# A decoder layer step: the recurrence's mean of squares as two split products

## The chip, the cores and the metric

The kernel runs on one core of a Trainium2 chip. The metric is device time in microseconds (us), the median of several runs; before the change it is 869.17 us (three runs, 868.96 to 870.31). Besides, one execution is recorded by the hardware profiler; all durations of single instructions come from that one.

## What is computed

One inference step of a decoder layer on 256 prompt tokens and 8 x 8 sample tokens, 320 rows of 2048. One projection of the rows feeds three groups of heads: sparse attention (8 heads, with an indexer that picks the keys, and pages of cached keys and values for the sample tokens), a gated linear recurrence (4 heads), and cross attention into memory (4 heads). Each branch is gated, the branches are concatenated and go through an output projection and a layer norm. The change concerns the recurrence's norm, which the reference writes so (`b_o` is the recurrence's output, 128 values a head and token):

```
bn = b_o * lax.rsqrt(jnp.mean(b_o * b_o, axis=-1, keepdims=True) + RMS_EPS) * norm_g
b = bn.reshape(n_b, n_t, W_B) * jax.nn.silu(bg)
```

## The kernel before

**The large products.** Activations stand transposed, features on the 128 partitions, the 320 tokens along the free axis. A float32 weight block (128x512) is split in two: ScalarE casts it to float32r (`wh`, line 626), VectorE or GpSimd subtracts to get the remainder (`wl`, lines 628 and 630). Each product is then three float32r matmuls, high by high, high by low, low by high (lines 1643 to 1645). In the profile these are the rows `pj<-xh,wh`, `pj<-xl,wh` and `pj<-xh,wl`. Other products, among them those of the recurrence, multiply float32 operands directly.

**The order.** Nearly every instruction passes through one helper (line 155), so the profile gives that line for all, and groups are told apart by tiles: `pj` are the projections' sums, `kv` and `va` the page visits' (scores and values), `mA` and `mB` the sums of the smaller stages, `t` and `bp` work buffers in SBUF, `pg` and `S` pages. While the program is built, a planner (class `Plan`, line 57, and the loop from line 2054) keeps an estimate of when each engine is free and each tile is ready. The branches' stages are generators (`bg`); at a `yield need(...)` a stage stops until the plan says that its operands are there, at `room` until a buffer is free, at `wait` until another stage has reported itself in `done`. Between the stages' steps the loop gives TensorE the next page visit (`unit`) or the next six matmuls of a projection (`pe_quantum`). `TT` (line 296) puts an elementwise operation on VectorE or on GpSimd, whichever the plan says is done first. The order within each engine is thus settled when the program is built, and every engine executes its own in that order.

**The recurrence** (`hgrn`, line 1333) treats its four heads one after the other. A head takes both large buffers `bp` (lines 1339 and 1340), transposes its values into the buffer `vN` (128x384, line 1346), builds decays and scores, then frees the two buffers and takes them again for the state `S0` and the sample tokens' values `vx` (line 1427). The decayed keys go into `kN` (128x256, line 1494). The head's output is formed in one sum `po` (lines 1522 to 1528), copied to `oT`, and squared by ScalarE into `sq` (line 1532). Eight updates of the state follow on VectorE (line 1540), the state is stored and its buffers freed (line 1543). The mean of the squares over the 128 partitions is a product with a constant matrix `onesm` whose entries are all 1/128 (line 1547), in float32. It leaves the mean in every partition. Lines 1549 to 1556 make the inverse root and scale.

`vN`, `kN` and `onesm` are single buffers; `onesm` is filled by a GpSimd memset at the start (line 1884). The masks' setup (`masks`, line 1926) runs after the indexer.

**The cross queries** of the sample tokens (`pad_queries`, line 439) need one `bp` buffer: it is cleared on GpSimd, ScalarE copies four heads' queries into it, and the visits `XK` to the memory keys read it. It is freed after the last visit `XV` (line 762).

Of the kernel before, what the change touches and what calls it, by code (L numbers as in the profile page):

```python
# [10 lines left out]
F32 = mybir.dt.float32  # L11
F32R = mybir.dt.float32r
# [4 lines left out]
OP = mybir.AluOpType  # L17
# [9 lines left out]
NS, NT = 64, 320  # L27
# [193 lines left out]
def need(*aps, ps=1, lag=0.0, visit=0.0):  # L221

    return (aps, ps, lag, visit)
# [3 lines left out]
def hymba_step(ctx: ExitStack, tc: tile.TileContext, I, O):  # L227
    nc = tc.nc
    plan = Plan()
    PE, ACT, DVE, POOL, SP = (Engine(plan, n, e) for n, e in (  # L230
        ("PE", nc.tensor), ("ACT", nc.scalar), ("DVE", nc.vector), ("POOL", nc.gpsimd), ("SP", nc.sync)))
# [7 lines left out]
    def new(shape, tag, dt=F32, p=None):  # L239
        uid[0] += 1  # L240
        bufs = BUFS.get(tag, 1)
        t = (p or pool).tile(shape, dt, name=f"{tag}_{uid[0]}", tag=tag, bufs=bufs)
        plan.slot(tag, bufs, t.tensor.name)
        if tag in ("t", "bp"):
            live[t.tensor.name] = [tag, 1]
        return t
# [7 lines left out]
    def free(*ts):  # L254
        for t in ts:
            e = live.get(t.tensor.name)
            if e:
                e[1] -= 1
                if e[1] == 0:
                    del live[t.tensor.name]  # L260

    def has_room(k, tag="t", spare=0):
        return sum(e[0] == tag for e in live.values()) + k + spare <= BUFS[tag]

    def room(k, tag="t", spare=0):
        while not has_room(k, tag, spare() if callable(spare) else spare):
            yield

    def const(shape, name, dt=F32):
        return pool.tile(shape, dt, name=name, tag=name, bufs=1)  # L270

    def T(cols=NT, dt=F32):
        return new([128, cols], "t", dt)
# [16 lines left out]
    def PS(shape, which=None, dt=F32):  # L290
        if which is None:
            fa, fb = [(held[w] == 2, plan.slot_free(w, 2)) for w in ("mA", "mB")]
            which = "mA" if fa <= fb else "mB"
        return new(shape, which, dt, psum)

    def TT(op, out, a, b):
        n = math.prod(out.shape[1:])
        d = max(plan.t["DVE"], plan.now) + (66 + n) / 960 + hold_dve[0]
        p = max(plan.t["POOL"], plan.now) + (170 + 2.0 * n) / 960
        (DVE if d <= p else POOL).tensor_tensor(out, a, b, op=op)  # L300
# [4 lines left out]
    def spare():  # L305
        return 0 if AQ else 0

    def store(dst, src):
        keep(src)
        outq.append((dst, src))  # L310
# [4 lines left out]
    ident = const([128, 128], "ident")  # L315
# [9 lines left out]
    ngt = const([128, 1], "ngt")  # L325
    eps = const([128, 2], "eps")
    one = const([128, 1], "one")
    onesm = const([128, 128], "onesm")
    emat = const([128, 2, 2, 2, 128], "emat", BF)
    pbias = const([128, 384], "pbias")  # L330
    maskb = const([128, HALF], "maskb", BF)
# [15 lines left out]
    done = set()  # L347
# [89 lines left out]
        return f  # L437

    def pad_queries():
        yield from wait(("mq", 0))  # L440
        yield from room(1, "bp")
        st["mqpad"] = x = new([128, 8, 4, 32], "bp")
        POOL.memset(x, 0.0)
        for h in range(4):
            yield from wait(("mq", h))
            q = st.pop(("mq", h))
            yield need(q, ps=0)
            ACT.copy(x[:, :, h, 8 * h:8 * h + 8], q[:, 256:320].rearrange("p (b t) -> p b t", b=8))
            free(q)
        done.add("mqpad")  # L450
# [363 lines left out]
    def wait(*keys):  # L814
        while not all(k in done for k in keys):
            yield
# [516 lines left out]
    def hgrn():  # L1333
        lb, olb = lbt[:, 8:12], lbt[:, 12:16]
        yield from wait("idxdone", "pbias", "masks")
        for h in range(4):
# [9 lines left out]
            vN = new([128, 3, 128], "vN")  # L1346
            ps = PS([128, 3, 128])
# [141 lines left out]
            ps = PS([128, 3, 128])  # L1489
# [1 line left out]
                PE.transpose(ps[:, i, :], kd[:, 128 * i:128 * i + 128], ident)  # L1491
            PE.transpose(ps[:, 2, :], kd[:, 192:320], ident)
            free(kd)
            kN = new([128, 2, 128], "kN")
            ACT.copy(kN, ps[:, 0:2])
            yield from room(3, spare=spare)
            kS = T(256, F32R)
# [6 lines left out]
            ps = PS([128, 2, 128])  # L1504
# [8 lines left out]
            for a in range(2):  # L1513
                for j in range(4):
                    PE.matmul(pq[32 * j:32 * j + 32, a, :], q[:, 256 + 32 * a:288 + 32 * a], S0[:, 4 * a + j, :],
                              start=True, stop=True)
# [13 lines left out]
            oT, sq = at, x  # L1530
            ACT.copy(oT, po)
            ACT.activation(sq, po, AF.Square)
            for a in range(2):
                yield need(vx, kS)
                ps = PS([128, 4, 128])
                PE.matmul(ps, kS[:, 0:128], vx[:, 4 * a:4 * a + 4, :], start=True, stop=False)
                PE.matmul(ps, kS[:, 128:256], vx[:, 4 * a:4 * a + 4, :], start=False, stop=True)
                for b in range(4):
                    e = 1 + 4 * a + b
                    DVE.scalar_tensor_tensor(S0[:, 4 * a + b, :], S0[:, 4 * a + b, :], eG[:, e:e + 1], ps[:, b, :],  # L1540
                                             op0=OP.mult, op1=OP.add)
            store(O["ss"][h], S0)
            free(S0, vx, kS)
            yield from room(1, spare=spare)
            yield need(sq)
            ps = PS([128, NT])
            PE.matmul(ps, onesm, sq, start=True, stop=True)
            y = T()
            ACT.activation(y, ps, AF.Ln, bias=eps[:, 0:1])
            ACT.activation(y, y, AF.Exp, scale=-0.5)  # L1550
# [330 lines left out]
        nc.tensor.matmul(warm_ps, warm[:, 0:128], warm, start=True, stop=True)  # L1881
    free(warm)
    POOL.memset(avS[0:64], 0.0)
    POOL.memset(onesm, 1.0 / 128)
    POOL.memset(one, 1.0)
    POOL.memset(eps[:, 0:1], RMS_EPS)
    POOL.memset(eps[:, 1:2], LN_EPS)
# [38 lines left out]
    def masks():  # L1926
        yield from wait("idxdone")
        yield from room(2, "bp")
        cm = [new([128, 1024], "bp"), new([128, 1024], "bp")]
        SP.dma_start(lbt[:, 0:8], I["lb"])  # L1930
        SP.dma_start(ngt, I["ng"])
        SP.dma_start(cm[0], I["cm"][:, 0:1024])
        SP.dma_start(cm[1], I["cm"][:, 1024:2048])
        yield need(*cm, lbt, ngt)
        ACT.copy(cu8, cm[0][:, 0:304])
        ACT.copy(emat.rearrange("p a b c d -> p (a b c d)"), cm[1])
        free(*cm)
        DVE.tensor_scalar(ngt, ngt, -0.5, None, op0=OP.mult)
        l0, l1, m = lbt[:, 0:4], lbt[:, 4:8], lbt[:, 8:12]
        DVE.tensor_max(m, l0, l1)  # L1940
        DVE.tensor_sub(l0, l0, m)
        DVE.tensor_sub(l1, l1, m)
        yield
        ACT.activation(lbt[:, 0:8], lbt[:, 0:8], AF.Exp)
        DVE.tensor_add(m, l0, l1)
        DVE.reciprocal(m, m)
        DVE.tensor_mul(lbt[:, 8:12], l0, m)
        DVE.tensor_scalar(lbt[:, 12:16], lbt[:, 8:12], -1.0, 1.0, op0=OP.mult, op1=OP.add)
        done.add("masks")


    for g in (setup(), masks(), idx_head(), idx_sample(), attn_scores(), attn_values(), *[new_keys(p) for p in range(4)],
              *[soft(p) for p in range(4)], hgrn(), pad_queries(), *[cross_prompt(h) for h in range(4)], split()):
        bg.append([g, None])
# [99 lines left out]
    while half < len(wspec) or bg or outq or later_in or pending or nunit < len(punits):  # L2054
        plan.now = max(plan.now, plan.t["PE"])
        loads()
        if pending and pending[0][0] is mem_values and has_room(4, spare=spare()):
            f, ps, _ = pending.pop(0)
# [8 lines left out]
        while pending and plan.avail(pending[0][1] if pending[0][2] == 3 else pending[0][1][-1]) <= plan.now \  # L2067
# [3 lines left out]
            f, ps, _ = pending.pop(0)  # L2071
# [138 lines left out]
```

## Time and profile before

| what | value |
|---|---|
| median of three runs | 869.17 us |
| lowest and highest | 868.96 and 870.31 us |
| the profiled execution's own time | 868.29 us |
| its span, first to last instruction | 866.5 us |
| mean granted TensorE clock | 0.998 |
| memory read and written | 256.50 and 8.73 MB |

The span is 1.79 us shorter than the time of the same execution. In the profile, PE is TensorE's matmuls and PEld its weight loads, DVE VectorE, ACT ScalarE, POOL GpSimd, SP the engine that issues most DMAs. A row of a timeline has start, duration, engine, line, operation, the tiles written and read, shape and number of instructions merged (`x2`); in square brackets stand the idle time before it and what ended it. A row of a group has busy time and mean duration in ns behind the bar, then idle time before these instructions and what ended most of it. A row of waits has who waited for whom, the time in total, how often, and the longest. Matmuls overlap, so their durations add up to more than the time that they take together.

### The profile page before, as it was taken

Reading aid. Unit: us, or ns where it says so; the run is one execution under the profiler, and the core shown is the slowest. Engines: PE = TensorE matmul, PEld = TensorE weight load, DVE = VectorE, ACT = ScalarE, POOL = GpSimd, SP = SyncE. Lnnn points to the kernel's source line nnn. Section 1 sums busy time; section 2 is a strip of 40 time slices with the busy share of each in tenths; the row PEclk is TensorE's granted clock in tenths of the full one; section 3 lists DMA queues with packets and bytes.
Section 4 is the critical chain, followed back from the end, with each engine's and each line's share of the span. In section 5 each row is a group of like instructions: output and inputs, shape, how many; then the busy total and the mean of one; then the engine's idle time right before and its main releaser. Section 6 shows DMA issues by size and latency. Waiting matters only on the chain.

```text
span 866.5 us, 19303 instructions
## 1 busy us (share of the span) xinstructions
PE 856.6 (99%) x6972; PEld 729.7 (84%) x6974; DVE 555.4 (64%) x1133; ACT 422.7 (49%) x900; POOL 299.1 (35%) x305
## 2 busy tenths in 40 slices
PE   9999999999999999999999999999999999999996
PEld 8999998888888998887878889677887789888885
DVE  6777989645888895563484448558635344953655
ACT  6444566544454545343463454555445353744432
POOL 0453553356544463040142213333411000623424
PEclk9999999999999999999999999999999999999999
DMA  8555644889999999999999999999999987856633
GB/s 306 185 176 159 183 140 129 326 310 371 398 384 385 346 358 363 363 377 406 380 350 399 400 367 381 403 405 362 379 372 395 373 334 257 297 174 195 194 98 122
DMA packets 84370, 266.51 MB, mean 308 GB/s; under 512 B 10609, under 2 KB 21810, under 8 KB 83634
## 3 DMA queue, kind: packets, MB, share of 16 engines
q1 hardware_dynamic: 83250, 263.18, 82.6%
q0 software_dynamic: 1024, 2.10, 0.8%
q8 instruction: 55, 0.90, 0.4%
q14 instruction: 41, 0.34, 0.1%
HBM read 256.50 MB, written 8.73 MB: 306 GB/s over the span
## 4 chain that ended last, share of the span: by engine, by line
PE 97%; DVE 1%; DMA 1%; SPq 0%; issue 0%; ACT 0%; DVEq 0%
PE pj L155 57%; PE mB L155 12%; PE va L155 10%; PE mA L155 10%; PE kv L155 8%; DMA pg<-in_xT 1%; DVE pg L155 0%; DVE t L155 0%; DVE s L155 0%; SPq L155 0%; DVE xl L155 0%; ACT xh L155 0%; DVE wl L155 0%; DVEq L2196 0%; DVE bns L155 0%
## 5 line engine op out<-in xcount | busy, mean ns | idle before, releaser
L155 ACT CAST wh<-wr 128x512 fp32r<-128x512 f32 x338 | 207.4, 619 | 255.7 <-PE pj L155 203.4
L155 PE MATMUL pj<-xh,wh 128*128 128x320 f32 x1008 | 322.0, 319 | 0.0
L155 PE MATMUL pj<-xh,wl 128*128 128x320 f32 x1008 | 311.5, 309 | 0.0
L155 PE MATMUL pj<-xl,wh 128*128 128x320 f32 x1008 | 311.3, 309 | 0.0
L155 DVE TENSOR_TENSOR wl<-wr,wh 128x512 fp32r<-128x512 f32 x239 | 181.9, 770 | 190.8 <-ACT wh L155 183.3
L155 POOL TENSOR_TENSOR wl<-wr,wh 128x512 fp32r<-128x512 f32 x99 | 131.8, 1335 | 235.4 <-ACT wh L155 217.9
L155 PEld LDWEIGHTS pj<-xh,wh 128*128 128x128 f32 x1008 | 189.4, 188 | 18.2 <-issue 13.5
L155 PEld LDWEIGHTS pj<-xl,wh 128*128 128x128 f32 x1008 | 189.5, 188 | 1.4
L155 PEld LDWEIGHTS pj<-xh,wl 128*128 128x128 f32 x1008 | 189.2, 188 | 0.0
L155 POOL TENSOR_TENSOR t<-t,t 128x320 f32<-128x320 f32 (+3 forms) x44 | 39.5, 898 | 129.6 <-ACT t L155 68.2
L155 PE MATMUL kv<-pg,qpad 128*32 128x256 f32 (+1 forms) x916 | 59.2, 380 | 0.0
L155 PE MATMUL va<-pg,PT 128*32 128x512 f32 x456 | 58.5, 595 | 0.0
L155 PEld LDWEIGHTS kv<-pg,qpad 128*32 128x32 f32 (+1 forms) x916 | 31.5, 110 | 21.1 <-issue 1.9
L155 DVE MAX8 PT<-PT 128x8 f32<-128x1032 f32 x32 | 39.5, 1233 | 0.5
L155 DVE MATCH_REPLACE8 PT<-PT 128x1032 f32<-128x1032 f32 x32 | 39.0, 1218 | 0.0
L155 PEld LDWEIGHTS va<-pg,PT 128*32 128x32 f32 x456 | 14.6, 109 | 29.0 <-issue 26.3
L155 POOL DMA_INDIRECT S<-in_ci,row x24 | 26.0, 1084 | 31.6 <-DVE row L155 22.0
L155 POOL TENSOR_TENSOR t<-t,tabm 128x320 f32<-128x320 f32 x16 | 14.1, 879 | 34.2 <-DVE t L155 32.6
L155 PE MATMUL mB<-t,wh 128*128 128x256 f32 x128 | 24.5, 290 | 0.0
L155 POOL TENSOR_TENSOR xl<-cat,xh 128x256 fp32r<-128x256 f32 x12 | 13.4, 1142 | 27.2 <-ACT xh L155 27.2
L155 POOL TENSOR_TENSOR bp<-t,bp 128x128 f32<-128x128 f32 (+1 forms) x17 | 10.4, 615 | 35.4 <-ACT bp L155 35.3
L155 ACT ACTIVATE S<-kv 128x512 f32<-128x512 f32 x16 | 9.5, 596 | 26.4 <-PE kv L155 23.2
(378 smaller groups left out, 1348.9 us busy)
## 6 DMA issues: line engine op xcount, KB each, us to landing
wr<-in_wt SPq DMA_DIRECT2D x126, 512.0 KB, 6.0
pg<-in_ck SPq DMA_DIRECT2D x114, 512.0 KB, 7.1
pg<-in_cv SPq DMA_DIRECT2D x114, 512.0 KB, 7.3
wr<-in_wo SPq DMA_DIRECT2D x36, 512.0 KB, 4.4
wr<-in_wm SPq DMA_DIRECT2D x16, 512.0 KB, 8.1
S<-in_ck SPq DMA_DIRECT2D x14, 512.0 KB, 6.8
S<-in_cv SPq DMA_DIRECT2D x14, 512.0 KB, 6.9
pg<-in_cXK SPq DMA_DIRECT2D x8, 512.0 KB, 9.4
```

Source lines behind the costliest of these rows:

```text
L155: res = f(*a, **k)
```

## The change

The squares are split into a float32r part `sh` and a float32r remainder `sl`, and the float32 product with `onesm` becomes two float32r products into one sum. No new buffers are made for the parts: `sh` takes the single buffer of the head's values (`vN`), `sl` that of its keys (`kN`), which becomes 128x320 for it. `onesm` becomes float32r, and is now written by a VectorE instruction in the masks' setup instead of the memset. The third head reports `states` when its state's buffers are free, and `pad_queries` waits for that besides the first cross query. ("Third" counts from zero: it is the last.)

```
-    onesm = const([128, 128], "onesm")
+    onesm = const([128, 128], "onesm", F32R)
...
     def pad_queries():
-        yield from wait(("mq", 0))
+        yield from wait(("mq", 0), "states")
         yield from room(1, "bp")
...
-            kN = new([128, 2, 128], "kN")
+            kN = new([128, NT], "kN")[:, 0:256].rearrange("p (a b) -> p a b", a=2)
...
             ACT.copy(oT, po)
             ACT.activation(sq, po, AF.Square)
+            sh, sl = new([128, 384], "vN", F32R)[:, 0:NT], new([128, NT], "kN", F32R)
+            ACT.copy(sh, sq)
+            TT(OP.subtract, sl, sq, sh.bitcast(F32))
...
             free(S0, vx, kS)
+            if h == 3:
+                done.add("states")
             yield from room(1, spare=spare)
-            yield need(sq)
+            yield need(sh, sl)
             ps = PS([128, NT])
-            PE.matmul(ps, onesm, sq, start=True, stop=True)
+            PE.matmul(ps, onesm, sh, start=True, stop=False)
+            PE.matmul(ps, onesm, sl, start=False, stop=True)
...
-    POOL.memset(onesm, 1.0 / 128)
...
+        DVE.tensor_scalar(onesm, ident, 0.0, 1.0 / 128, op0=OP.mult, op1=OP.add)
```

## Prediction

> **What bounds the kernel now.** I read the page first: its busy times, its forty slices and the chain that ended last.
>
> ```profile
> span 866.5 us, 19303 instructions
> PE 856.6 (99%) x6972; PEld 729.7 (84%) x6974; DVE 555.4 (64%) x1133; ACT 422.7 (49%) x900; POOL 299.1 (35%) x305
> PE 97%; DVE 1%; DMA 1%; SPq 0%; issue 0%; ACT 0%; DVEq 0%
> ```
>
> TensorE is busy for 99% of the span and carries 97% of the chain. Matmuls overlap, so "busy" alone could hide waiting; hence the second view, who TensorE waited for, asked for that engine alone. Its two longest rows:
>
> ```profile
> PE kv L1881 <- DVE t L155: 1.1, 1, 1.1
> PE mB L155 <- DVE t L155: 0.3, 1, 0.3
> ```
>
> The first is the start of the program; after it TensorE waits next to nothing. The third view is busy time by stage, for the stretch in which the recurrence works and the one around its end:
>
> ```profile
> 350.00:650.00 300.00, 299.93 (x2847) 244.13 (x2849) 169.54 (x354) 144.91 (x321) 80.64 (x98) 1.00 1.00 382
> 650.00:716.00 66.00, 65.73 (x524) 50.86 (x523) 30.11 (x75) 30.75 (x79) 6.35 (x6) 1.00 0.93 362
> ```
>
> The columns are the stretch's length, then PE, PEld, DVE, ACT and POOL busy, the granted clock, the DMA share and GB/s. TensorE fills both stages (299.93 of 300.00 us, 65.73 of 66.00), at a granted clock of 1.00. The DMA engines are full too from 350 to 650, but no wait of TensorE's comes of it, since projections stand ready between the page visits. So what counts is the time for which TensorE's stream is occupied; work on the other engines counts only if it makes that stream wait or puts it into another order.
>
> **The change part by part.** *The product itself.* Before, each head multiplies the squares by a constant 128x128 matrix in full float32. The tile view of that constant, two rows of it:
>
> ```profile
> L155 PE MATMUL mA<-t,onesm x6: 431/432/433, 509.9 to 680.2; 128*128 128x320 f32 x6
> L155 PE MATMUL mB<-t,onesm x2: 432/432/433, 433.9 to 434.2; 128*128 128x320 f32 x2
> ```
>
> Eight instructions for four heads: one product of the program is two on the engine. What it occupies is not the 432 ns (instructions overlap) but the distance between starts, in TensorE's timeline around the second head, and in a piece of the chain that holds projections alone:
>
> ```profile
> 509.61 0.31 PE L155 MATMUL pj<-xl,wh 128*128 128x320 f32 x1
> 509.75 0.31 PE L155 MATMUL pj<-xh,wl 128*128 128x320 f32 x1
> 509.90 0.70 PE L155 MATMUL mA<-t,onesm 128*128 128x320 f32 x2
> 510.20 0.55 PE L155 MATMUL pj<-xh,wh 128*128 128x320 f32 x1
> 510.59 0.31 PE L155 MATMUL pj<-xl,wh 128*128 128x320 f32 x1
> ```
>
> ```profile
> 718.25 22.88 PE pj L155 x156
> ```
>
> From the last projection matmul before it (509.75) to the second one after it (510.59) are 0.84 us. That holds two projection matmuls, 128x128 by 128x320 in float32r, which otherwise follow each other at 22.88 / 156 = 0.147 us. So the full float32 product takes 0.84 - 2 x 0.147 = 0.55 us. After the change it is two float32r products of the projections' shape: 2 x 0.147 = 0.29 us. Saved: 0.25 us a head, 1.0 us for four. This is the first term, and it lies on TensorE, on the path.
>
> Does the stream of matmuls set that distance, or the loading of their weights? The loads' timeline at the same place:
>
> ```profile
> 509.61 0.19 PEld L155 LDWEIGHTS pj<-xh,wl 128*128 128x128 f32 x1
> 509.76 0.34 PEld L155 LDWEIGHTS mA<-t,onesm 128*128 128x128 f32 x2
> ```
>
> There are two loads a product before and two after. Loads of 0.19 us stand 0.15 us apart, so they overlap one another, and 0.34 us of loads do not explain a product of 0.55 us. I take the stream as the limit, and 1.0 us as the term. The Trainium skill's "Perfetto Trace Analysis", in its section Identifying the Most-Contended Engine, would have TensorE's distance from its limit judged by the share of the weight loads and not by busy matmuls. By that measure, 84% here and untouched by the edit, the term would be nothing, and the sum the old time. The steady 0.147 us under loads of 0.19 speak against it here.
>
> *The split.* Each head gets a cast of the squares on ScalarE (line 1532's result into the buffer of the values) and a subtraction on VectorE or GpSimd. The nearest groups by form, of the same shape and number types, then the two ends for the constant:
>
> ```profile
> L155 ACT CAST PT<-S 128x320 fp32r<-128x320 f32 x4 | 1.8, 457 | 1.1 <-DMA S<-in_wik 1.1
> L155 DVE TENSOR_TENSOR cat<-S,PT 128x320 fp32r<-128x320 f32 x4 | 1.9, 486 | 2.6 <-ACT PT L155 2.6
> L155 POOL TENSOR_TENSOR t<-t,t 128x320 f32<-128x320 f32 x19 | 17.3, 910 | 71.8 <-DVE t L155 24.7 <-PE pj L155 17.3 <-ACT t L155 14.9
> L155 DVE TENSOR_SCALAR pbias<-pbias 128x128 f32<-128x128 f32 x1 | 0.2, 228 | 0.0
> L155 POOL MEMSET onesm<- 128x128 f32 x1 | 0.2, 198 | 0.0
> ```
>
> So 4 x 0.46 = 1.8 us more on ScalarE (49% busy), and 4 x 0.49 = 1.9 us more on VectorE (64%) or 4 x 0.91 = 3.6 us on GpSimd (35%). The constant moves from a 0.2 us memset at the program's start to a 0.2 us VectorE instruction in the masks' setup, after the indexer. All of this runs beside TensorE's stream: I put it at nothing, with the stream's other work as its cover.
>
> *What the split delays.* The head's own chain is longer by 0.46 + 0.49 = 0.94 us, or 0.46 + 0.91 = 1.37 us with GpSimd. Here is head 3: ScalarE's square,
>
> ```profile
> 678.55 0.45 ACT L155 ACTIVATE t<-mB 128x320 f32<-128x320 f32 x1
> ```
>
> then VectorE's first four state updates and TensorE's product:
>
> ```profile
> 678.75 1.12 DVE L155 SCALAR_TENSOR_TENSOR bp<-bp,eG,mA 128x128 f32<-128x128 f32 x4 [0.61 <-PE mA L155]
> ...
> 679.89 0.70 PE L155 MATMUL mA<-t,onesm 128*128 128x320 f32 x2
> ```
>
> The square ends at 679.00 and the product starts at 679.89, so 0.89 us of the extra 0.94 to 1.37 are there already; the rest only moves the product behind some projection matmuls, because the planner issues it when its estimate says that both parts are there. Behind the subtraction on VectorE stand the eight state updates: the first starts at 678.75 now and at 679.00 + 0.94 = 679.94 then, 1.2 us later. Who waits for those: the state's store and the release of two large buffers, and then the cross queries.
>
> *The parts' buffers.* They take the values' and keys' single buffers, whose readers (the keys' and values' products) stand before the square in the same head; the next head's copy into them stands after the product. I see no new wait in that, at worst one that the sequence of the head has anyway.
>
> *The wait for the states.* The cross queries' buffer is one of the two large ones, both held by head 3 until its states are done. ScalarE's rows of head 3's first exponentials and of the first cross query's copy, GpSimd's of the clearing of its buffer, ScalarE's of the last query's copy, and the chain's piece with the visit that reads them:
>
> ```profile
> 594.57 0.83 ACT L155 ACTIVATE t<-t 128x320 f32<-128x320 f32 x2
> ...
> 617.37 0.42 ACT L155 COPY t<-pj 128x320 f32<-128x320 f32 x1
> ...
> 683.19 0.95 POOL L155 MEMSET bp<- 128x1024 f32 x1
> ...
> 686.70 0.24 ACT L155 COPY bp<-t 128x64 f32<-128x64 f32 x1
> ...
> 697.09 3.59 PE kv L155 x64
> ```
>
> Head 3 holds both buffers from 594.57; the first cross query is there at 617.37, 23 us later; the buffer is cleared at 683.19, after the states. The new wait is thus one that already takes place, and costs nothing. With the states 1.2 us later the padded queries are there at some 688.1 instead of 686.94, still 9 us ahead of the visit at 697.09 that needs them. And if that visit slipped, the 22.88 us of projections from 718.25, with no visit among them, are there to fill the stream. Without that cover each microsecond of delay would cost one.
>
> The sum: 868.29 us (profiled execution: span 866.5 and 1.79 around it) - 1.01 = 867.28. That execution lies 0.88 under the median of the runs, 869.17; carried over to it, 869.17 - 1.01 = 868.16, my forecast 868.2. The runs before span 0.16%; I take 0.2% (1.74 us) as what can be told from no change.
>
> **The unknown cost** is the order. The kernel's order is planned by estimated times; from the masks on every estimate of VectorE shifts by a fraction of a microsecond, from the first head on TensorE's and ScalarE's too, and choices made by a comparison may fall otherwise. Two prices for that, TensorE's timeline at a product whose operand came later than planned, and at the entry into a page visit:
>
> ```profile
> 651.26 0.33 PE L155 MATMUL mB<-ident,t 128*128 128x128 f32 x1
> 651.87 0.55 PE L155 MATMUL mB<-ident,t 128*128 128x128 f32 x3 [0.27 <-DVE t L155]
> ...
> 681.17 0.31 PE L155 MATMUL pj<-xh,wl 128*128 128x320 f32 x1
> 681.41 1.92 PE L155 MATMUL va<-pg,PT 128*32 128x512 f32 x16
> ```
>
> The late operand cost 0.61 us between two starts where a transpose needs under 0.2 (three end within 0.55), so 0.4 to 0.5; a visit's entry takes 0.24 instead of 0.147, 0.1, and I allow as much for its exit. A handful of each, either way, is an estimate of 1 to 2.3 us of either sign. I take zero, since nothing in the trace favours a sign.
>
> **The rivals.** *The gain does not arrive* (0.10): TensorE is limited by loading weights or by the pages, and the product's shortening is filled with waiting. For it: DMA at 1.00 from 350 to 650, and two weight loads a product before and after, the measure that "Perfetto Trace Analysis" would go by. Against it: the loads overlap, as shown, and TensorE lacks 0.07 us of 300 in just that stretch, so it waits for no page. The time would be the old one, 869.2.
>
> *The order falls better* (0.28): two late operands fewer, or some visits merged, bring 0.8 to 2.3 us beyond the term: 865.9 to 867.4, faster.
>
> *TensorE stands at the product* (0.06): its queue is in order, and if a part is later than the plan thinks, the projections behind it wait. Each head loses its gain at 0.25 us of such waiting; over 0.2% slower needs (1.74 + 1.01) / 4 = 0.69 us in each. If cast and subtraction lay wholly on TensorE's path, 4 x 1.37 = 5.5 us: 868.2 + 5.5 = 873.7. Against it: the planner waits for both parts, and the error of its estimates seen above is 0.5 us, in a single place.
>
> *The order falls worse* (0.05): 2.8 us or more lost, six late operands: 870.9 or over.
>
> **How the numbers follow.** The forecast, order about kept, has the remaining 0.51. Faster by over 0.2% (under 867.4) is the better order: 0.28. Within 0.2%: forecast and lost gain, 0.61. Slower: the standing product and the worse order, 0.11. The range is the forecast with 2.3 us of order below and 2.4 above: 865.9 to 870.6. It leaves out the tails of the last two rivals and some of the better order, about 2 in 10. The forecast's own part is about 867.5 to 868.9.
>
> **What would show it.** In the profile after: the matmuls with the constant still eight, but at 0.15 us between starts, 0.25 us less a head from the projection before to the one after; the cast at about 0.46 us and the subtraction at 0.49 or 0.91; first state update about 1.2 us after the square; the clearing of the cross buffer right behind the states; TensorE still at 99%, the pieces of pure projections at the end about as long. Wrong I would be if TensorE's row of waits shows the constant's product with a wait of 0.3 us or more, if the page visits split into more pieces than before, or if the stream of TensorE has the same or a greater sum of gaps than the 1 us saved.

## The result, and the profile after

The changed kernel takes 874.51 us, the median of five runs (872.73 to 875.23), beside 869.17 us for the kernel before on the same chip: ratio 1.0055, 95% interval 1.0043 to 1.0066. It is 5.3 us slower, and lies outside the range of the prediction, on the side that had a chance of 0.11. The profiled execution took 874.51 us, its span is 872.7 us. (Other chips gave the kernel before 867.85, 869.64 and 868.09 us. So experiments are compared by their ratio to runs of before on their own chip.)

The page, with the lines that answer to the first ones of before, shows little: TensorE is still busy for 98% of the span, but 6.2 us of span have come on top.

```profile
span 872.7 us, 19322 instructions
PE 858.7 (98%) x6972; PEld 731.0 (84%) x6974; DVE 559.0 (64%) x1125; ACT 423.2 (49%) x904; POOL 312.5 (36%) x317
PE 94%; DVE 2%; POOL 1%; issue 1%; DMA 1%; ACT 1%; SPq 0%; DVEq 0%; POOLq 0%; ACTq 0%
```

The second view, who TensorE waited for, has a row that before has not:

```profile
PE mB L155 <- ACT t L155: 3.3, 1, 3.3
PE kv L1887 <- DVE t L155: 1.1, 1, 1.1
PE pj L155 <- DVE wl L155: 0.8, 1, 0.8
```

The third row, a wait at 86 us ahead of all of the change's work, is no part of the change (see the last section); it adds about 1 us to the difference between these two profiles. The first row is the one that counts: a single wait of 3.3 us. It is not at the product over the squares, but at matmuls that write a bank `mB`. TensorE's timeline at that place, of the kernel after:

```profile
612.66 0.31 PE L155 MATMUL pj<-xh,wl 128*128 128x320 f32 x1
616.30 0.55 PE L155 MATMUL mB<-ident,t 128*128 128x128 f32 x3 [3.33 <-ACT t L155]
616.60 0.43 PE L155 MATMUL pj<-xh,wh 128*128 128x320 f32 x1
616.83 0.46 PE L155 MATMUL pj<-xl,wh 128*128 128x320 f32 x1
617.09 0.47 PE L155 MATMUL pj<-xh,wl 128*128 128x320 f32 x1
...
620.02 0.41 PE L155 MATMUL pj<-xl,wh 128*128 128x320 f32 x1
620.27 0.31 PE L155 MATMUL pj<-xh,wl 128*128 128x320 f32 x1
620.42 0.32 PE L155 MATMUL pj<-xh,wh 128*128 128x320 f32 x1
```

The three merged instructions are head 3's transposes of its values (line 1346 and after). They stand at the head of TensorE's queue, which is in order, and projections that need nothing from them stand behind. Two things are to be seen. First the stop itself. Second, what follows it: projection matmuls that start every 0.147 us elsewhere start every 0.266 us from 616.83 to 620.27, 13 of them, which is 13 x 0.12 = 1.55 us more. The busy time by stage says why (length, PE, PEld, DVE, ACT and POOL busy, then the granted clock):

```profile
612.00:617.00 5.00, 1.67 (x12) 1.41 (x11) 4.69 (x8) 2.58 (x8) 2.73 (x2) 0.98 0.81 269
617.00:624.00 7.00, 7.00 (x40) 7.00 (x39) 2.29 (x2) 2.10 (x5) 2.57 (x2) 0.77 0.94 293
```

In the seven microseconds behind the stop TensorE is full, and its granted clock is 0.77, where it was 1.00 in the stages of before. Stop and slow stretch are 3.3 + 1.55 = 4.9 us of the 5.3.

What did the transposes wait for? The other engines' timelines in those microseconds:

```profile
612.24 1.37 DVE L155 TENSOR_TENSOR wl<-wr,wh 128x512 fp32r<-128x512 f32 x1 [1.48 <-ACT wh L155]
613.53 1.54 DVE L155 SCALAR_TENSOR_TENSOR t<-t,ngt,t 128x320 f32<-128x320 f32 x1
...
615.42 0.75 DVE L155 COPY t<-mB 128x256 f32<-128x256 f32 x2
...
615.87 0.70 ACT L155 COPY t<-mB 128x256 f32<-128x256 f32 x2 [2.42 <-DVE t L155]
...
611.76 2.96 POOL L155 TENSOR_TENSOR wl<-wr,wh 128x512 fp32r<-128x512 f32 x2 [2.19 <-ACT wh L155]
```

The four copies `t<-mB` move the memory keys out of the two banks `mB`, which the memory projection has just filled. VectorE makes two of them, and is late. Beside GpSimd's splitting of weights its own split takes 1.37 us instead of 0.69, and the gate's step 1.54, where one of its shape at 608 us takes 0.55. ScalarE's two copies come behind VectorE's. Only then is a bank free for the transposes. In the kernel before, the same transposes stood 17 us earlier, in the other kind of bank:

```profile
595.36 0.49 PE L155 MATMUL mA<-ident,t 128*128 128x128 f32 x3
```

And the product that the change is about? Here is head 1's, in TensorE's timeline of after:

```profile
511.69 0.31 PE L155 MATMUL pj<-xh,wl 128*128 128x320 f32 x1
511.84 0.31 PE L155 MATMUL mA<-vN,onesm 128*128 128x320 f32 x1
511.99 0.31 PE L155 MATMUL mA<-kN,onesm 128*128 128x320 f32 x1
512.14 0.31 PE L155 MATMUL pj<-xh,wh 128*128 128x320 f32 x1
512.29 0.31 PE L155 MATMUL pj<-xl,wh 128*128 128x320 f32 x1
```

From 511.69 to 512.29 are 0.60 us, where before had 0.84 between the same neighbours: 0.24 us less, as forecast. So the loss does not come from the product's price. The orders of all engines are the same as before up to head 0's product at 434 us (but for the constant's write) and differ from there on.

### The profile page after: what moved, and what is told of

Its sections match the earlier page's. It is cut to its first block, busy times and chain, and to the rows that moved or that the text cites. A ratio compares the mean times of both kernels' runs of the same rounds, so it can differ in the third digit from the quotient of the medians.

```text
span 872.7 us, 19322 instructions
## 1 busy us (share of the span) xinstructions
PE 858.7 (98%) x6972; PEld 731.0 (84%) x6974; DVE 559.0 (64%) x1125; ACT 423.2 (49%) x904; POOL 312.5 (36%) x317
## 4 chain that ended last, share of the span: by engine, by line
PE 94%; DVE 2%; POOL 1%; issue 1%; DMA 1%; ACT 1%; SPq 0%; DVEq 0%; POOLq 0%; ACTq 0%
PE pj L155 55%; PE mB L155 12%; PE va L155 10%; PE mA L155 9%; PE kv L155 8%; DMA pg<-in_xT 1%; POOL S L155 1%; DVE wl L155 1%; DVE pg L155 1%; DVE t L155 1%; POOL t L155 0%; POOL pg L155 0%; DVE cat L155 0%; ACT t L155 0%; SPq L155 0%
## 5 line engine op out<-in xcount | busy, mean ns | idle before, releaser
L155 POOL TENSOR_TENSOR wl<-wr,wh 128x512 fp32r<-128x512 f32 x102 | 137.7, 1355 | 210.7 <-ACT wh L155 207.6
L155 POOL TENSOR_TENSOR t<-t,t 128x320 f32<-128x320 f32 (+3 forms) x49 | 43.9, 896 | 118.6 <-ACT t L155 71.6
L155 ACT ACTIVATE t<-t 128x320 f32<-128x320 f32 (+1 forms) x44 | 18.5, 455 | 8.6 <-DVE t L155 8.4
L155 PEld LDWEIGHTS mB<-t,wh 128*128 128x128 f32 x128 | 20.7, 190 | 1.1
```

Of the source, the lines that this page charges most:

```text
L155: res = f(*a, **k)
```

## The experiments

My theory when they began: the new order of the instructions costs the time, by the one collision at 613 us. The rivals: the split or the product itself costs it, or any new order would.

**The change's instructions in the old order.** The planner is told the old costs, so it writes before's order; the new instructions are put in beside it.

```
+            sh, sl = new([128, 384], "vN", F32R)[:, 0:NT], new([128, NT], "kN", F32R)
+            nc.scalar.copy(sh, sq)
+            nc.gpsimd.tensor_tensor(sl, sq, sh.bitcast(F32), op=OP.subtract)
...
-            PE.matmul(ps, onesm, sq, start=True, stop=True)
+            nc.tensor.matmul(ps, onesm, sh, start=True, stop=False)
+            nc.tensor.matmul(ps, onesm, sl, start=False, stop=True)
+            plan.run("PE", PE.cost("matmul", [ps], [ident, sq], NT), [ps], [onesm, sq])
```

> The changed kernel's instructions (cast, subtraction on GpSimd, two float32r products, the constant on VectorE) in the order of the kernel before: the planner is told the old costs, so every engine's list is the old one with the new instructions put in. If the order is what costs (theory A), the term of 0.25 us a head is all that is left: 868.2 us, 867.7 to 868.9. If the instructions themselves cost (theory B: the split, or TensorE standing at the product), it is as slow as the changed kernel, 874 us, and TensorE's waits name the product.

Measured: ratio 1.0020 (1.0011 to 1.0029). Most of the loss is gone, but the gain is not there. TensorE's waits in that kernel say why:

```profile
PE mA L1551 <- POOL kN L1535: 0.6, 2, 0.3
PE mB L155 <- ACT t L155: 0.5, 1, 0.5
PE pj L155 <- ACT qpad L155: 0.4, 1, 0.4
PE mB L1551 <- POOL kN L1535: 0.3, 1, 0.3
```

At three heads TensorE stands 0.3 us at the low part's product (line 1551 there). Measured between the same neighbours as before, from 510.02 to 511.17 us at head 1, such a product takes 1.15 us in place of 0.84: 0.3 more than the full product, instead of 0.25 less. The idle time that a row names understates the cost, since a matmul's row is longer (0.31 us) than the distance to the next one (0.147). The wait of 0.5 us, at 619 us, is new as well; that of 0.4 us stands at 7 us, ahead of the change's work, and also in a kernel below (`stop_1_and_3us`) that has before's instructions there. The old order left no time for the split on GpSimd.

**The old instructions in the new order.** The full product without a split, in the order of the change.

```
-            PE.matmul(ps, onesm, sh, start=True, stop=False)
-            PE.matmul(ps, onesm, sl, start=False, stop=True)
+            nc.tensor.matmul(ps, onesm, sq, start=True, stop=True)
+            for s in (sh, sl):
+                plan.run("PE", PE.cost("matmul", [ps], [sh[:, 0:128], s], NT), [ps], [onesm, s])
```

> The other way round: the full float32 product of the kernel before, no split, in the changed kernel's order. Theory A: the changed kernel's 874.5 us and the 1.0 us of the product on top, 875.5 us, with TensorE's stop near 613 us and the slower matmuls after it still there. Theory B: the kernel before, 869.2 us.

Measured: 1.0069 (1.0056 to 1.0083), with the same stop of 3.3 us and a slow stretch behind it. So the order costs, with or without the new instructions.

**Head 3's transposes elsewhere.** Two kernels of the change itself: the transposes in a bank `mA`, or planned 4 us later.

```
+            while h == 3 and n_free("mA") == 0:
+                yield
             vN = new([128, 3, 128], "vN")
-            ps = PS([128, 3, 128])
+            ps = PS([128, 3, 128], "mA" if h == 3 else None)
```

> The changed kernel, but the three transposes of the last head's values go into the other pair of sum buffers (mA), which the memory projection does not use. If TensorE's 3.3 us stop is the wait for the memory keys' copies out of mB (theory A), it goes, and with it the 3.4 us of slower matmuls behind it (1.6 us lost): 869.6 us, 869 to 871. If the transposes wait for their own operand or for the head's chain, the stop stays and so does 874.5 us.

> The changed kernel, but the last head's transposes are planned 4 us later, so that TensorE has projections in front of them while the copies run. Theory A: the stop of 3.3 us is gone or under 0.5 us, 869.6 us, 869 to 871.5 as the order behind it shifts too. If the stop is of the chain of that head and not of the buffer, it moves along and the time stays at 874 us.

Measured: 1.0005 (0.9995 to 1.0014) and 1.0029 (1.0016 to 1.0041). In both, the stop is gone, so it hangs on that one meeting. In the second, no other large wait takes its place; the order behind changes as well, so that its remaining 2.6 us have no single cause that I could name.

**Another order, for another reason.** Before's instructions; only the planner is told that the product takes 0.243 us less.

```
-            PE.matmul(ps, onesm, sq, start=True, stop=True)
+            nc.tensor.matmul(ps, onesm, sq, start=True, stop=True)
+            plan.run("PE", PE.cost("matmul", [ps], [ident, sq], NT) - 0.243, [ps], [onesm, sq])
```

> The instructions of before, all of them; only the planner is told that the product over a head's squares takes 0.243 us less than it thinks, and so it writes another order behind head 0's product (200 lines of TensorE's order differ). Theory (the loss of the change is one coincidence in its order, head 3's transposes set ahead of the memory keys' copies): no stop over 1 us at the memory keys' bank, ratio 0.998 to 1.003. Rival (the planner's order of before is a lucky one and any other draw costs several us): ratio 1.004 or more.

Measured: 0.9998 (0.9989 to 1.0007). A quarter of a microsecond in one estimate gives another order (TensorE's differs from 580 us on), and that costs nothing measurable here. So a new order need not cost anything; this is one draw, and it leaves the first two thirds as they were.

**The split on VectorE, in the old order** (`nc.vector` for `nc.gpsimd` in the first experiment's edit).

> The change's own instructions in the order of before, as in new_ops_old_order, but the subtraction that makes the low part is put on VectorE instead of GpSimd. Theory (in the old order the gain of 1.0 us was eaten by TensorE standing 0.3 us at the low part of three heads, because GpSimd takes 0.88 us for the subtraction): VectorE takes some 0.5 us, the stand at the low product falls from 0.9 us in all to under 0.3, and the ratio to before comes to 0.999 to 1.000 (new_ops_old_order: 1.0020). Rival (VectorE's queue is no shorter there: state updates and split weights stand in it): the stand stays at 0.2 to 0.3 us a head or moves to the high product, the ratio stays at 1.001 to 1.003.

Measured: 1.0003 (0.9994 to 1.0012). The stand at the low part is gone, and one of 0.6 us at head 2's high part has come. In TensorE's timeline there:

```profile
590.30 0.39 PE L1550 MATMUL mA<-vN,onesm 128*128 128x320 f32 x1 [0.62 <-DVE bp L155]
590.53 0.31 PE L1551 MATMUL mA<-kN,onesm 128*128 128x320 f32 x1
```

Here the parts are not late: the cast ends at 588.60 us and the subtraction at 589.12. The product waits for its bank `mA`, from which VectorE's first four state updates read until 590.15, and these now stand behind the subtraction. The prediction had seen that the updates would come later, but not that a bank hangs on them. The rival of the prediction that TensorE stands at the product exists in the old order, by a late part or a late bank, at 0.3 to 0.6 us where it happens. In the change's own order it does not: there the planner had moved the product behind some projections, and its waits have no row of it.

**A stop by itself.** Before, with small multiplications by one on idle GpSimd put between two quanta of pure projections, at two places, so that TensorE stops there; no instruction of TensorE is added.

```
+            tq.append(K)
+            n = {498: 2, 508: 6}.get(len(tq), 0)     # 4 and 11 in the second kernel
+            for m in range(n):
+                e = xh[:, K if m == n - 1 else K - 1, 0:64]
+                nc.gpsimd.tensor_tensor(e, e.bitcast(F32), one[:, 0:1].broadcast_to([128, 64]), op=OP.mult)
```

> The kernel before with two stops of TensorE put into the stretch of pure projections at about 720 and 729 us: two and then six small multiplications by one of a slice of the activations on GpSimd, which is idle there, each 0.57 us by the nearest row, between two quanta of projections that read that slice: stops of about 1.3 and 3.6 us, no instruction of TensorE added. Theory (an idle TensorE of over 3 us makes the chip grant a lower clock, and the matmuls behind it start every 0.27 us instead of every 0.147 for some 3.4 to 5.2 us): the second stop is followed by such a stretch, the first is not; time over before 4.9 us of stops and 1.6 to 2.4 us behind: 6.5 to 7.3 us. Rival (the slow matmuls in the changed kernel came from what ran beside them, late operands or transfers): no slow stretch here, 4.9 us.

> As stop_1_and_3us with four and eleven multiplications: stops of about 2.5 and 6.5 us. Theory (lower granted clock behind a stop): a slow stretch of 1.6 to 2.4 us of loss behind the second, and if the point lies under 2.5 us behind the first too: 9 us and 1.6 to 4.8 us more, 10.6 to 13.8 us over before. Rival (no clock, other work): 9 us.

The multiplications took 0.37 us each and not 0.57, so the stops came out at 0.8 and 2.3 us, and at 1.6 and 4.1 us. Measured: 1.0052 (1.0038 to 1.0065) and 1.0094 (1.0079 to 1.0109). TensorE's timeline behind the stop of 2.3 us:

```profile
734.88 0.41 PE L155 MATMUL pj<-xh,wh 128*128 128x320 f32 x1 [2.29 <-POOL xh L1645]
735.13 0.31 PE L155 MATMUL pj<-xl,wh 128*128 128x320 f32 x1
735.28 0.30 PE L155 MATMUL pj<-xh,wl 128*128 128x320 f32 x1
```

and behind that of 4.1 us, with the stages' busy time and granted clock (0.59 and 0.55) below it:

```profile
736.68 0.41 PE L155 MATMUL pj<-xh,wh 128*128 128x320 f32 x1 [4.14 <-POOL xh L1645]
736.93 0.30 PE L155 MATMUL pj<-xl,wh 128*128 128x320 f32 x1
...
737.62 0.47 PE L155 MATMUL pj<-xh,wl 128*128 128x320 f32 x1
737.88 0.47 PE L155 MATMUL pj<-xh,wh 128*128 128x320 f32 x1
...
740.55 0.42 PE L155 MATMUL pj<-xl,wh 128*128 128x320 f32 x1
740.81 0.31 PE L155 MATMUL pj<-xh,wl 128*128 128x320 f32 x1
```

```profile
737.00:739.00 2.00, 2.00 (x11) 2.00 (x10) 0.49 (x1) 0.62 (x1) 0.00 (x0) 0.59 0.00 0
739.00:741.00 2.00, 2.00 (x10) 2.00 (x10) 0.20 (x1) 0.00 (x0) 0.00 (x0) 0.55 0.41 61
```

Behind 2.3 us of idleness the matmuls are at full pace at once, and so behind 0.8 and 1.6. Behind 4.1 us they start every 0.266 us from 737.62 to 740.81. So a stop alone brings the slow stretch, also among pure projections, and also when GpSimd ends it and not ScalarE.

Its length alone does not decide, though. `old_ops_new_order` has the same stop of 3.3 us as the change, and there the slow stretch begins sooner. Two rows of TensorE's timeline in that kernel, then two stages with the granted clock (0.63 and 0.50):

```profile
611.74 0.31 PE L155 MATMUL pj<-xh,wl 128*128 128x320 f32 x1
615.39 0.90 PE L155 MATMUL mB<-ident,t 128*128 128x128 f32 x3 [3.34 <-ACT t L155]
```

```profile
614.00:615.00 1.00, 0.00 (x0) 0.00 (x0) 0.97 (x5) 0.04 (x1) 0.00 (x0) 0.63 0.78 225
616.00:618.00 2.00, 2.00 (x10) 2.00 (x9) 1.68 (x1) 0.66 (x2) 1.28 (x1) 0.50 1.00 345
```

The clock is 1.00 up to 614 us, and 0.63 over the next microsecond: it falls to half at about 614.3, when TensorE has stood for 2.2 us and has 1.1 still to stand. So 2.2 us of idleness were enough here, while 2.3 were not enough above. It also differs between runs of one program. Of the change's five runs, one has a mean granted clock of 0.998, as before has, and takes 872.73 us; three have 0.996 and 874.12 to 874.69 us; one has 0.993 and 875.23 us. The first seems to have had no slow stretch, the last a longer one. Of the five runs of `stop_1_and_3us`, one of 875.00 us has 0.995, so a stop of 2.3 us may be followed by one too.

The Trainium skill's "TensorE: Matmul & The Clock Gate", in its section What's actually happening, gives the rule: the array's clock falls to half after an idle window of some 3.4 us and comes back after a busy one, the windows running freely. The traces agree in the half (granted 0.50, 0.266 us between starts instead of 0.147), and free windows would explain why the same stop is answered differently from run to run. They do not agree in the length: some 2.2 us of idleness were enough in one kernel.

**The planner's wrong entry.** Why did the planner put the transposes into a bank that was still full? Its book of live banks (`slot`, line 72) drops the tile with the oldest last use when a new one is taken. The memory projection takes both `mB` banks in one line (1655 before). A new tile takes over the last use of the one that it replaces, until it is written. So when the second bank is taken, the first still has the oldest time in the book, and it is the one that is dropped, not the dead tile from an earlier stage. From then on the book shows one bank `mB` that nobody uses. While both are held, nothing asks for it; when the memory projection ends, the transposes do. One line mends the entry:

```
-                pj["m"] = [PS([128, 512], w) for w in ("mB", "mB", "pj", "pj")]
+                pj["m"] = []
+                for w in ("mB", "mB", "pj", "pj"):
+                    pj["m"].append(PS([128, 512], w))
+                    plan.w[plan.key(pj["m"][-1])] = plan.now
```

With it, the change's orders stay as they are on every engine, except that head 3's three transposes and the copy of their result name `mA` instead of `mB`.

> The change, with one line more in the planner's book: each of the four banks that the memory projection takes is entered as in use from the moment it is taken. Without it the planner drops the first of the two mB banks from its list of live banks when it takes the second (never written, it counts as the oldest), so that at 613 us it holds one mB bank for free that the memory keys still fill. The orders of all engines are those of the change, but for one thing: head 3's transposes of values go to a bank mA instead of mB. Theory (this wrong entry is what made the loss): no stop over 1 us at 612 to 617 us, granted clock 1.0 there, some 5 us less than the changed kernel, ratio to before 0.999 to 1.001. Rival (the transposes are too early in any bank, their input or the copy behind them is late): a stop of over 1 us stays, ratio 1.002 or more.

> As bank_book, in the same order of all engines, but with the old full product and without the split (as old_ops_new_order). Theory (in this order the product's matmuls are worth what the rows say and nobody waits for the split): 1.0 us slower than bank_book, 0.25 us later from each head's product on. Rival (the gain is taken back by waits for the parts): within 0.3 us of bank_book.

> The kernel before with the same line in the planner's book; 42 lines of TensorE's order change, all behind the memory projection. Theory (before had the same wrong entry, but no work met it): ratio 0.999 to 1.001, no stop over 0.5 us new. Rival (before pays for it too): 0.998 or less.

Measured: `bank_book` 1.0006 (0.9996 to 1.0015), `old_ops_book` 1.0014 (1.0005 to 1.0023), `before_book` 0.9998 (0.9989 to 1.0007). In `bank_book` the transposes go through where the stop was, and the clock stays:

```profile
611.90 0.31 PE L155 MATMUL pj<-xh,wl 128*128 128x320 f32 x1
612.05 0.49 PE L155 MATMUL mA<-ident,t 128*128 128x128 f32 x3
612.29 0.39 PE L155 MATMUL pj<-xh,wh 128*128 128x320 f32 x1
```

```profile
617.00:624.00 7.00, 7.00 (x58) 4.99 (x60) 6.90 (x9) 3.33 (x7) 3.75 (x4) 1.00 0.95 359
```

A bank's name alone is worth 0.49% (1.0055 less 1.0006; with the two intervals 0.3 to 0.6%), some 4.3 us. The two traces have one order, so they can be laid side by side: from the last projection ahead of the transposes to the fifteenth behind them are 2.53 us in `bank_book` (611.90 to 614.43) and 7.61 in after (612.66 to 620.27), 5.1 more. And in one and the same order, the split product is worth 869.26 - 868.41 = 0.85 us by the medians; the intervals of the two ratios overlap, and the spans of the two profiles differ by 867.3 - 866.6 = 0.7. Before has the wrong entry too, but no work meets it.

**The late copies.** The change with its stop left in, but all four memory-key copies on ScalarE, the planner told the old engines.

```
-            (ACT.copy if h % 2 else DVE.tensor_copy)(t, acc[h // 2][:, 256 * (h % 2):256 * (h % 2) + 256])
+            src = acc[h // 2][:, 256 * (h % 2):256 * (h % 2) + 256]
+            nc.scalar.copy(t, src)
+            e = ACT if h % 2 else DVE
+            plan.run(e.name, e.cost("copy" if h % 2 else "tensor_copy", [t], [src], 256), [t], [src])
```

> The change, its wrong entry and its stop left in; only the two memory-key copies that VectorE makes are made by ScalarE, with the planner told the old engines, so that the orders of the other engines stay. Theory A (the copies are late because VectorE's queue is: its split of a weight and the gate's step stand beside GpSimd's split of weights and take 1.37 and 1.54 us instead of 0.69 and 0.55): ScalarE is free at 613.5 us, the four copies end by 614.7, the stop falls from 3.3 to about 1.7 us, and since the stops of 0.8 and 2.3 us had no slow stretch behind them, no matmuls at 0.27 us follow: 3 us less than the changed kernel, ratio 1.002. Theory B (the copies wait for a buffer that VectorE's earlier step sets free): they still start at 615.5 us, stop 3.3 us and slow stretch stay, ratio 1.005 to 1.006.

Measured: 1.0011 (1.0002 to 1.0020). TensorE's wait there, then ScalarE's row:

```profile
PE mB L155 <- ACT t L1737: 1.1, 1, 1.1
```

```profile
612.45 1.18 ACT L1737 COPY t<-mB 128x256 f32<-128x256 f32 x4
```

ScalarE's copies start 0.7 us after the last projection ahead of the transposes (at 611.74) and wait for nothing; in the change they start 3.2 us after it (612.66). So it was VectorE's queue that they had waited behind. The stop is 1.1 us, and the granted clock is 1.00 behind it. With VectorE's lateness taken away, the planner's wrong entry thus still costs a stop of 1.1 us; the other 2.2 us of the stop, and the slow stretch, came by the lateness.

## Why the prediction was wrong

**What bounds the kernel: right.** TensorE's stream still sets the time, and the time for which it stood was lost, with the slow stretch on top.

**The product: right in kind, a little too high in size.** The forecast was 1.0 us. The distance in the stream is 0.24 us less at head 1, 4 x 0.24 = 0.96 us, and two kernels of one order differ by 0.85 us. So *the gain does not arrive* falls as it was meant: weight loads do not set the product's price. (The section of the Trainium skill's "Perfetto Trace Analysis" that the prediction names judges TensorE by two measures, the share of the weight loads and the share of the peak arithmetic rate; the prediction took the first alone.)

**The split put at nothing: right in this order, and for the reason given.** The durations were 0.46 us (cast) and 0.88 us (subtraction, GpSimd at all four heads) as forecast:

```profile
L155 ACT CAST vN<-t x4: 460/460/461, 434.0 to 685.4; 128x320 fp32r<-128x320 f32 x4
L155 POOL TENSOR_TENSOR kN<-t,vN x4: 884/884/887, 434.5 to 686.0; 128x320 fp32r<-128x320 f32 x4
L155 DVE TENSOR_SCALAR onesm<-ident x1: 1331/1331/1331, 209.9 to 209.9; 128x128 fp32r<-128x128 f32 x1
```

The planner moved the product behind projections, as the prediction expected. In the old order, which left no room for that, TensorE stood 0.3 us at three heads. The first state update did not move by 1.2 us, since the subtraction took GpSimd; and the constant took 1.33 us and not 0.2, off the path.

**The waits for the states and for the parts' buffers: right.** Taking the wait for the states out of the change, or putting it alone into before, leaves the instruction order of every engine as it was, and no row of TensorE's waits names it. The parts' buffers have no row either.

**The step that failed: the unknown cost of the order.** It said: "A handful of each, either way, is an estimate of 1 to 2.3 us of either sign. I take zero." The price came from two rows, a late operand of 0.27 us of waiting, 0.4 to 0.5 in all, and the entry into a page visit, 0.1, and *the order falls worse* was thought of as six of those and given 0.05. The order without its collision did cost 869.26 - 868.05 = 1.2 us (`old_ops_book` against `before_book`, by the medians; 0.4 to 2.0 us by the interval of its ratio), inside that estimate. What was not in it is a single operand that is 3.3 us late, because the planner's book is wrong about a bank, with a stretch at half clock behind. In the sum: 0.85 us gained, 1.2 lost to the order, 3.3 + 1.55 lost at the stop, makes 5.2 of the 5.3 us. That it comes so close is partly luck, since the first two are known to about a microsecond only. Even without the collision the change is not faster: `bank_book` is at 1.0006, where the forecast of 868.16 us would be 0.9988. Of the prediction's three signs of being wrong the last one came: the gaps in TensorE's stream grew by more than the 1 us saved, while no wait names the product.

Could it have been seen before? Not the meeting itself, for the trace has no row of it. But two things stood in the code and the profile: that banks `mB` come free in one place, behind copies on a VectorE that is 64% busy, and that the planner never learns how late an engine really is. An error of the plan at a bank that a whole stage has held is not bounded by the waits of a run in which it didn't happen. That bound was the mistake, more than the sign.

What stays open is which of the planner's decisions brought head 3's transposes 17 us later in the new order. I have not followed it decision by decision.

None of the twelve kernels beats before by more than can be measured. A product in the old order, moved far enough behind the parts, might keep its 0.9 us; that is not shown, since it wasn't tried.

## What to carry to other kernels

Where an order is planned by estimates, a change of a quarter of a microsecond can draw a new order. Price that by the largest stop that an in-order queue can meet (a bank held by a whole stage, copied out by a busy engine), not by the waits that the old order shows. To tell an edit's own worth from the order's, run the old instructions in the new order and the new ones in the old. And when one row of the waits holds nearly all the loss, ask the planner's book why it thought that the operand was there.

## What the runs showed of the hardware

**A stop of TensorE can cost more than its length.** Behind stops of 3.3 us (two kernels) and 4.1 us, the granted clock is 0.50 for a while: for 3.4 us in the change and behind the stop of 4.1 us, for some 6.8 us in `old_ops_new_order`, where it fell 1.1 us before the restart. The projections then start every 0.266 us instead of every 0.147. That is 1.5 to 2.5 us on top of the stop. Behind stops of 0.8 to 2.3 us no profile shows it. Where the point lies cannot be given as one length, as the runs of one program differ.

**GpSimd blocks VectorE for whole instructions.** The constant's 1.33 us, and the instructions behind it in VectorE's timeline of after, stand beside GpSimd's splits, two of which run from 209.80 to 212.40:

```profile
209.90 1.33 DVE L155 TENSOR_SCALAR onesm<-ident 128x128 fp32r<-128x128 f32 x1
...
211.21 1.21 DVE L155 TENSOR_TENSOR lbt<-lbt 128x4 f32<-128x4 f32 x1
```

Four columns took 1.21 us. The Trainium skill's "SBUF — State Buffer", in its section Who interferes with whom, says that an instruction of VectorE with two inputs in SBUF contends with one of GpSimd that reads SBUF, that one of the constant's kind can too in some modes, and that the pair of ports which they share is locked exclusively. The rows agree: these two instructions end at 211.23 and 212.42 us, the second right behind the split that ends at 212.40. So do those at 612 to 615 us, where it made the copies late.

**A wait that comes and goes with the run.** TensorE's wait of 0.7 to 0.8 us for `wl` at 86 us, in a part that is the same in all these kernels, stands in the profile of after and in all four on the chip where before takes 869.64 us, and in none of the other kernels' profiles. It moves all behind it by 1.0 us (after against `bank_book`), of the 1.6 to 1.8 us by which before is slower on that chip than on the two others of the experiments. What brings it is not known; it is no part of the change.
